# More seven-product pairs in a SwiGLU on Trainium2, with activation sums kept in DRAM

## The chip, the cores and the metric

The kernel runs on one core of one Trainium2 chip. The metric is device time in microseconds (us). The kernel before takes 2040.8 us, the median of three runs (2040.3 to 2041.55). Lower is better. A profile was taken of one more execution.

The engines have short names here: PE is TensorE (matmuls), PEld its weight loads, DVE is VectorE, ACT is ScalarE, POOL is GpSimd and SP is the engine that issues most DMAs. All five run their own instructions in the order in which the program put them there, and wait for each other through semaphores.

## What is computed

A two-layer encoder on 256 tokens of width 2048, with 256 memory tokens. Each layer has a token mixer (a gated MLP in layer 0, attention in layer 1), attention into the memory, an output projection, and a dense SwiGLU of inner width 5632. Everything is float32. The change touches the SwiGLU alone:

```python
D_MODEL = 2048; SEQ = 256; DEPTH = 2; D_FF = 5632
def swiglu(h, w_gate_up, w_down):
    gate, up = jnp.split(h @ w_gate_up, 2, axis=-1)
    return (jax.nn.silu(gate) * up) @ w_down
def reference(...):
    for l in range(DEPTH):
        ...
        x = x + jnp.concatenate([tok_out, mem_out], axis=-1) @ w_out[l]
        x = x + swiglu(rms_norm(x, g_ffn[l]), w_gate_up[l], w_down[l])
    return x
```

## The kernel before

**Precision.** PE multiplies in fp32r, a shortened float32. To keep precision, each operand is split into a high and a low part, `hi` and `lo`: ACT makes `hi` by a cast (L254 for weights), DVE makes `lo` by a subtraction (L255). Each product of a 128-row block is then three matmuls (`matmul3`, L198 to L200): hi by hi, lo of the activations by hi, hi by lo of the weights.

**Pairs.** In the feed-forward stage a `Pair` computes two blocks of 512 output columns at once for both halves of the tokens. For gate/up the two blocks are gate and up of one block `f` of the inner width (11 of them, "pair f"), for down they are two neighbouring blocks of the output (two pairs, `jj` = 0 and 1, for each chunk of the inner width). A pair runs over units: a unit `i` covers two blocks of 128 features, so gate/up has 8 units, down 8 (or 6 in the last chunk). Its weights, four tiles of 128x512, come in as `raw` by two DMAs of SP (L357).

**Eight or seven products.** A unit is a 2x2 by 2x2 product of blocks. `eight` does it with 8 products, 24 matmuls. `seven` does it with 7 products, 21 matmuls, as Strassen's method does (in Winograd's form). For this it needs sums of weights, which DVE forms in `prepare` (L347 to L350, four additions, the three new ones in a tile `T`) and which are split too (a second pair of `whi` and `wlo`, of 1536 elements), and sums of activations (`activation_sums`, L300 to L308: four short DVE instructions and a split). At the end of the last seven of a pair, `inner` combines four PSUM banks (a copy on ACT and four DVE additions, L397 to L401; in down four more, L405). At the end of the last unit, `outer` adds the other four banks (L413, two after each half of the tokens).

**Which units are seven.** In gate/up units 0, 1 and 2 of the features (`fast`, L743), two of them in pair 0 and three in all others; their activation sums are made once a layer and lie in SBUF. In down the units in `quick` (L762): two in the first two chunks for either `jj`, and in the last chunk none in layer 0 and one in layer 1. The lists `order` say where in the pair the sevens stand: with three sevens in gate/up they are units one, three and five of eight.

**What sets the order.** The code issues unit after unit and prepares one unit ahead (`run`, L327 to L337). Other work is put in by a queue of delays, `later` and `tick` (L96 to L112), one tick for each half unit: the transposes and splits of the SwiGLU output (`turn_a`), the residuals and so on. A scheduler then orders the instructions of each engine. There are three buffers of `whi` and three of `wlo` (`W_TILES`), four of `raw`, four PSUM banks `acc` and four `m`, and 26 tiles `a` for activations, sums and products in the feed-forward stage (`FFN_TILES`).

Of the kernel before, what the change touches and what calls it, by code (L numbers as in the profile page):

```python
# [10 lines left out]
F32 = mybir.dt.float32  # L11
F32R = mybir.dt.float32r
AF = mybir.ActivationFunctionType
ALU = mybir.AluOpType
AX = mybir.AxisListType

P = 128
# [10 lines left out]
NB = 512  # L28
# [3 lines left out]
KC4 = 4  # L32
# [4 lines left out]
KC3 = 3  # L37


class Parts:  # L40
# [8 lines left out]
    def get(self, kc, t):  # L49
        return self.ap[kc, t]  # L50
# [3 lines left out]
def encoder(ctx: ExitStack, tc: tile.TileContext, x, mem, g_mix, g_ffn, w_in_a, g_v_a, w_spatial, b_spatial,  # L54
            w_in_b, g_q_b, g_k_b, g_mem, w_mem_kv, g_mq, g_mk, w_out, w_gate_up, w_down, rope_c, rope_s, out):
    nc = tc.nc
# [7 lines left out]
    dram = ctx.enter_context(tc.tile_pool(name="dram", bufs=1, space=bass.MemoryType.DRAM))  # L64
# [6 lines left out]
    def nm(s):  # L71
        uid[0] += 1
        return f"{s}_{uid[0]}"

    def big(dt=F32, shape=None):
        return room["p"].tile(shape or [P, NB], dt, tag="a", name=nm("a"))

    def small(n, long=False):
        return sp.tile([P, n], F32, tag=f"{'r' if long else 's'}{n}", name=nm(f"s{n}"), bufs=8 if long else 6)

    def misc():
        return psm.tile([P, NB], F32, tag="m", name=nm("m"))

    def v4(a):
        return a.rearrange("p (c n) -> p c n", n=P)
# [10 lines left out]
    def later(delay, fn):  # L96
        queue.append((clock[0] + delay, len(queue), fn))

    def tick():
        clock[0] += 1  # L100
        run_due(clock[0])
# [86 lines left out]
    def split(src, shape):  # L188

        hi = big(F32R, shape)  # L190
        lo = big(F32R, shape)
        nc.scalar.copy(hi, src)  # L192
        nc.vector.tensor_tensor(lo, src, hi.bitcast(F32), ALU.subtract)  # L193
        return hi, lo
# [7 lines left out]
    def transpose4(src, dst):  # L202
        for c in range(4):
            nc.tensor.transpose(dst[:, c * P:(c + 1) * P], src[:, c * P:(c + 1) * P], ident)  # L204
# [27 lines left out]
    class Norm:  # L232


        def __init__(self):
            self.ss = [small(8, long=True) for _ in range(NT)]
# [11 lines left out]
    def halves(raw, n, step=KC4):  # L248

        hi = wp.tile([P, KC4, NB], F32R, tag="whi", name=nm("whi"))[:, :n]  # L250
        lo = wp.tile([P, KC4, NB], F32R, tag="wlo", name=nm("wlo"))[:, :n]
        for c in range(0, n, step):
            cut = slice(c, min(c + step, n))
            nc.scalar.copy(hi[:, cut], raw[:, cut])  # L254
            nc.vector.tensor_tensor(lo[:, cut], raw[:, cut], hi[:, cut].bitcast(F32), ALU.subtract)  # L255
        return [(hi[:, c, :], lo[:, c, :]) for c in range(n)]
# [43 lines left out]
    def activation_sums(a0, a1):  # L300

        q = big(F32, [P, 4, P])
        nc.vector.tensor_tensor(q[:, 0], a1[:, 0], a1[:, 1], ALU.subtract)
        nc.vector.tensor_tensor(q[:, 2], a1[:, 0], a0[:, 0], ALU.subtract)
        nc.vector.tensor_tensor(q[:, 1], a0[:, 0], q[:, 0], ALU.subtract)
        nc.vector.tensor_tensor(q[:, 3], a0[:, 1], q[:, 1], ALU.subtract)
        hi, lo = split(q, [P, 4, P])
        return [(hi[:, i, :], lo[:, i, :]) for i in range(4)]  # L308

    class Pair:  # L310

# [27 lines left out]
        def prepare(self, i):  # L339

            if i in self.ready:
                return
            raw = self.fetch(i)
            self.ready[i] = (raw,)
            if i in self.fast:
                T = room["p"].tile([P, KC3, NB], F32, tag="T", name=nm("T"), bufs=2)
                nc.vector.tensor_tensor(raw[:, 0], raw[:, 0], raw[:, 1], ALU.add)  # L347
                nc.vector.tensor_tensor(T[:, 0], raw[:, 0], raw[:, 3], ALU.add)
                nc.vector.tensor_tensor(T[:, 1], T[:, 0], raw[:, 1], ALU.subtract)
                nc.vector.tensor_tensor(T[:, 2], T[:, 0], raw[:, 2], ALU.add)  # L350
                self.ready[i] = raw, T

        def fetch(self, i):
# [11 lines left out]
            matmul3(self.bank[name], a, b, self.part[name] == 1, self.part[name] == self.of.get(name, self.most))  # L365

        def seven(self, i, raw, T):
            t1, w00, w10, w11 = halves(raw, KC4)
            t2, t3, t4 = halves(T, KC3)
            get, (q5, s2, q7, q3) = self.parts.get, self.sums[i]  # L370
            k0, k1 = 2 * i, 2 * i + 1
            inner = [(1, get(k0, 0), w00), (5, q5, t1), (6, s2, t2), (7, q7, t3)]
            outer = [(2, get(k1, 0), w10), (3, q3, w11), (4, get(k1, 1), t4)]
            if self.bank:
                inner, outer = inner[:1] + outer[:2], inner[1:] + outer[2:]
            for some in (inner, outer):
                for name, a, b in some:
                    self.add(name, a, b)
                tick()
# [225 lines left out]
    for l in range(DEPTH):  # L605
# [105 lines left out]
        else:  # L711
# [12 lines left out]
            for c in range(3):  # L724
                acc = linear(hT, w, c * NB)
                attend(head_norm(acc, norm.r, ghead["q"], True), (5, 6, 10, 13), lambda: own["k"], lambda: own["v"],
                       lambda h, c=c: (4 * c + h) // 3, 4 * c, cat)
# [12 lines left out]
        scope = ExitStack()  # L740
        room["p"] = scope.enter_context(tc.tile_pool(name=f"ffn{l}", bufs=FFN_TILES, reuse_waits="tile"))
        sums = {}
        fast = (0, 1, 2)  # L743

        def feature_sums(i):
            j, c = i // 2, 2 * (i % 2)
            whole = []
            for t in range(NT):
                hi, lo = hF.whole[j, t]
                a = big(F32, [P, 2, P])  # L750
                nc.vector.tensor_tensor(a, hi[:, c:c + 2].bitcast(F32), lo[:, c:c + 2].bitcast(F32), ALU.add)
                whole.append(a)
            sums[i] = activation_sums(*whole)

        for i in fast:
            later(2 + 2 * i, lambda i=i: feature_sums(i))

        hT = Parts()
        next_norm = Norm()
        for chunk in (range(0, 4), range(4, 8), range(8, 11)):  # L760
            aT, aS, half = Parts(), {}, {}
            quick = [2 * f + 1 for f in chunk[:2 if chunk[-1] < 10 else l]]  # L762

            def turn_a(a, t, f, aT=aT, aS=aS, half=half, quick=quick):
                tp = misc()
                transpose4(a, tp)
                hi, lo = split(v4(tp), [P, 4, P])
                for i in range(4):
                    aT.put(4 * f + i, t, hi[:, i, :], lo[:, i, :])
                i = 2 * f + 1  # L770
                if i in quick:
                    half[i, t] = big(F32, [P, 2, P])
                    nc.scalar.copy(half[i, t], v4(tp)[:, 2:4])
                    if t == NT - 1:
                        aS[i] = activation_sums(half[i, 0], half[i, 1])

            pairs = {}
            for f in chunk:
                order, some = ((3, 4, 5, 0, 6, 1, 7, 2), 2) if f == 0 else ((0, 3, 1, 4, 2, 5, 6, 7), 3)
                pairs[f] = Pair(hF, sums, w_gate_up[l], f * NB, DFF + f * NB, order, fast[:some])  # L780
            for f, g in pairs.items():
                g.run(pairs.get(f + 1))
                for t in range(NT):
                    a = kp.tile([P, NB], F32, tag="sg", name=nm("sg"), bufs=2)
                    nc.scalar.activation(a, g.out[t][0], AF.Silu, scale=norm.r[t])
                    nc.vector.scalar_tensor_tensor(a, g.out[t][1], norm.r[t], a, ALU.mult, ALU.mult)
                    later(3 + t if f == chunk[-1] else 12 + t, lambda a=a, t=t, f=f: turn_a(a, t, f))
            last = chunk[-1] == 10
            every = [2 * f + c for f in chunk for c in range(2)]
            slow = [i for i in every if i not in quick]  # L790
            pairs = []
            for jj in range(2):
                order = list(slow)
                for n, i in enumerate(quick):
                    order.insert(2 * n + (0 if jj and not last else 2), i)
                into = [[X[t][2 * jj + n] for n in range(2)] for t in range(NT)]
                pairs.append(Pair(aT, aS, w_down[l], 2 * jj * NB, (2 * jj + 1) * NB, order, quick, into))
            for jj, g in enumerate(pairs):
                g.run(None if jj else pairs[1])
                for j in (2 * jj, 2 * jj + 1):  # L800
                    if last and l < DEPTH - 1:
                        residual_turns(j, next_norm, gslice("mix", l + 1), hT)
                    elif last:
                        for t in range(NT):
                            parts = 2 if j == 3 and t == NT - 1 else 1
                            for i in range(parts):
                                cs = slice(i * NB // parts, (i + 1) * NB // parts)
                                eng = nc.scalar if i else nc.sync
                                eng.dma_start(out[0, t * P:(t + 1) * P, j * NB + cs.start:j * NB + cs.stop],
                                              X[t][j][:, cs])  # L810
# [37 lines left out]
```

## Time and profile before

| | |
|---|---|
| median of 3 runs | 2040.8 us (2040.3 to 2041.55) |
| span of the profiled execution | 2038.5 us |
| HBM read / written | 390.26 MB / 4.19 MB |
| granted PE clock | 1.000 |
| weight units split on DVE (2048 elements) | 264 |
| halves T split on DVE (1536 elements) | 82 |

The span runs from the first to the last instruction of the profiled execution; nothing else of that execution is timed, so its own time stands beside the median by the span alone, 2.3 us shorter. In the rows of the profile a group reads: line, engine, operation, output<-input, shapes, count | busy us in all, mean ns of one | idle time of its engine ahead of it and what ended it. In rows of a timeline the first two numbers are start and duration in us. In rows of waits: who <- whom: us in all, times, the longest.

### The profile page before, as it was taken

Reading aid. Unit: us, or ns where it says so; the run is one execution under the profiler, and the core shown is the slowest. Engines: PE = TensorE matmul, PEld = TensorE weight load, DVE = VectorE, ACT = ScalarE, POOL = GpSimd, SP = SyncE. Lnnn points to the kernel's source line nnn. Section 1 sums busy time; section 2 is a strip of 40 time slices with the busy share of each in tenths; the row PEclk is TensorE's granted clock in tenths of the full one; section 3 lists DMA queues with packets and bytes.
Section 4 is the critical chain, followed back from the end, with each engine's and each line's share of the span. In section 5 each row is a group of like instructions: output and inputs, shape, how many; then the busy total and the mean of one; then the engine's idle time right before and its main releaser. Section 6 shows DMA issues by size and latency. Waiting matters only on the chain.

```text
span 2038.5 us, 24693 instructions
## 1 busy us (share of the span) xinstructions
PE 2027.7 (99%) x9298; PEld 1679.9 (82%) x9298; DVE 1605.0 (79%) x1862; ACT 1095.0 (54%) x1389; POOL 50.6 (2%) x80
## 2 busy tenths in 40 slices
PE   9999999999999999999999999999999999999999
PEld 7888888888888888888888888888888888888887
DVE  5675557998879988887566886589979899798876
ACT  7765455454445554444555765555544455444552
POOL 2010000000000000000010100000000000000000
PEclk9999999999999999999999999999999999999999
DMA  9754554646656465665566544555566555565554
GB/s 325 253 179 155 185 188 154 227 165 206 203 190 227 165 207 196 202 227 194 186 198 204 173 133 141 202 185 178 195 206 218 195 184 190 205 221 192 183 197 137
DMA packets 202432, 396.08 MB, mean 194 GB/s; under 512 B 11068, under 2 KB 11432, under 8 KB 202312
## 3 DMA queue, kind: packets, MB, share of 16 engines
q1 hardware_dynamic: 198800, 385.79, 56.6%
q0 software_dynamic: 2048, 6.42, 1.0%
q10 hardware_dynamic: 1464, 2.28, 0.3%
q8 instruction: 73, 1.20, 0.2%
q14 instruction: 47, 0.39, 0.1%
HBM read 390.26 MB, written 4.19 MB: 194 GB/s over the span
## 4 chain that ended last, share of the span: by engine, by line
PE 96%; DVE 3%; DMA 1%; issue 1%; ACT 0%; SPq 0%; DVEq 0%; ACTq 0%
PE acc L200 27%; PE acc L199 27%; PE acc L198 27%; PE m L200 4%; PE m L198 4%; PE m L199 4%; PE m L204 2%; DVE wlo L255 1%; DMA raw<-in_w_gate_up 1%; PE m L500 0%; PE m L643 0%; ACT whi L254 0%; DVE x L413 0%; DVE e L413 0%; DMA x<-in_x 0%
## 5 line engine op out<-in xcount | busy, mean ns | idle before, releaser
L254 ACT CAST whi<-raw 128x2048 fp32r<-128x2048 f32 (+2 forms) x465 | 700.8, 1539 | 585.0 <-PE acc L199 512.5
L255 DVE TENSOR_TENSOR wlo<-raw,whi 128x2048 fp32r<-128x2048 f32 (+2 forms) x465 | 836.4, 1823 | 223.9 <-ACT whi L254 220.1
L198 PE MATMUL acc<-whi,h 128*128 128x512 f32 x1440 | 563.7, 392 | 0.0
L199 PE MATMUL acc<-whi,h 128*128 128x512 f32 x1440 | 562.6, 391 | 0.0
L200 PE MATMUL acc<-wlo,h 128*128 128x512 f32 x1440 | 524.1, 392 | 0.9 <-DVE wlo L255 0.9
L198 PE MATMUL acc<-whi,a 128*128 128x512 f32 x1062 | 414.8, 391 | 0.0
L199 PE MATMUL acc<-whi,a 128*128 128x512 f32 x1062 | 414.2, 390 | 0.0
L200 PE MATMUL acc<-wlo,a 128*128 128x512 f32 x1062 | 398.2, 391 | 0.0
L200 PEld LDWEIGHTS acc<-wlo,h 128*128 128x128 f32 x1440 | 270.6, 188 | 56.6 <-DVE wlo L255 1.5
L199 PEld LDWEIGHTS acc<-whi,h 128*128 128x128 f32 x1440 | 270.7, 188 | 55.3
L198 PEld LDWEIGHTS acc<-whi,h 128*128 128x128 f32 x1440 | 271.0, 188 | 54.0
L200 PEld LDWEIGHTS acc<-wlo,a 128*128 128x128 f32 x1062 | 199.4, 188 | 41.3 <-DVE wlo L255 0.3
L199 PEld LDWEIGHTS acc<-whi,a 128*128 128x128 f32 x1062 | 199.5, 188 | 40.4
L198 PEld LDWEIGHTS acc<-whi,a 128*128 128x128 f32 x1062 | 199.5, 188 | 40.2
L254 ACT CAST whi<-T 128x1536 fp32r<-128x1536 f32 x82 | 121.4, 1480 | 143.8 <-PE acc L199 102.2
L255 DVE TENSOR_TENSOR wlo<-T,whi 128x1536 fp32r<-128x1536 f32 x82 | 143.5, 1750 | 39.1 <-ACT whi L254 39.0
L198 PE MATMUL m<-whi,a 128*128 128x512 f32 x264 | 104.2, 395 | 0.7 <-ACT whi L254 0.7
L199 PE MATMUL m<-whi,a 128*128 128x512 f32 x264 | 102.9, 390 | 0.0
L347 DVE TENSOR_TENSOR raw<-raw 128x512 f32<-128x512 f32 x82 | 56.1, 684 | 54.9 <-DMA raw<-in_w_gate_up 53.5
L200 PE MATMUL m<-wlo,a 128*128 128x512 f32 x264 | 89.6, 389 | 0.0
L192 ACT CAST a<-m 128x512 fp32r<-128x512 f32 x80 | 46.7, 587 | 42.8 <-PE m L204 31.7
L193 DVE TENSOR_TENSOR a<-m,a 128x512 fp32r<-128x512 f32 x80 | 53.8, 682 | 13.1 <-ACT a L192 12.9
(126 smaller groups left out, 1473.1 us busy)
## 6 DMA issues: line engine op xcount, KB each, us to landing
raw<-in_w_gate_up SPq DMA_DIRECT2D x352, 512.0 KB, 4.7
raw<-in_w_down SPq DMA_DIRECT2D x176, 512.0 KB, 5.2
raw<-in_w_out SPq DMA_DIRECT2D x32, 1024.0 KB, 5.1
raw<-in_w_in_a SPq DMA_DIRECT2D x24, 1024.0 KB, 5.2
raw<-in_w_in_b SPq DMA_DIRECT2D x24, 1024.0 KB, 5.1
raw<-in_w_mem_kv SPq DMA_DIRECT2D x16, 1024.0 KB, 5.1
raw<-in_w_in_a SPq DMA_DIRECT2D x7, 512.0 KB, 6.2
x<-in_x SPq DMA_DIRECT2D x8, 256.0 KB, 5.8
```

The lines of the kernel that those rows point to most:

```text
L192: nc.scalar.copy(hi, src)
L193: nc.vector.tensor_tensor(lo, src, hi.bitcast(F32), ALU.subtract)
L198: nc.tensor.matmul(out, lhsT=a[0], rhs=b[0], start=start, stop=False)
L199: nc.tensor.matmul(out, lhsT=a[1], rhs=b[0], start=False, stop=False)
L200: nc.tensor.matmul(out, lhsT=a[0], rhs=b[1], start=False, stop=stop)
L204: nc.tensor.transpose(dst[:, c * P:(c + 1) * P], src[:, c * P:(c + 1) * P], ident)
L254: nc.scalar.copy(hi[:, cut], raw[:, cut])
L255: nc.vector.tensor_tensor(lo[:, cut], raw[:, cut], hi[:, cut].bitcast(F32), ALU.subtract)
L347: nc.vector.tensor_tensor(raw[:, 0], raw[:, 0], raw[:, 1], ALU.add)
```

## The change

- Gate/up has a fourth unit of seven products, i = 3 (`fast`), which pairs 2, 5, 7 and 9 use (`many`); they then alternate seven and eight to the end, `(0, 4, 1, 5, 2, 6, 3, 7)`. The others keep their two or three.
- Down has three sevens for `jj` = 1 in the first two chunks (`some`), and one in the last chunk for `jj` = 0 (in layer 1 for both). In all 13 units more are sevens.
- The activation sums of gate/up are written to DRAM when they are made (`spilt`), by POOL's DMA queue, and read back into new tiles during the second half of down, for the next chunk (`reload_sums`).
- The sums of weights take three DVE instructions in place of four: one of 2x512 elements and two of 512 (now L352 to L354). The products 5 and 6 change places in `inner` of `seven`.

```diff
+    class Quarters(list):
+        def __init__(self, hi, lo):
+            self.tiles = hi, lo
+            super().__init__((hi[:, i, :], lo[:, i, :]) for i in range(4))
...
             if i in self.fast:
                 T = room["p"].tile([P, KC3, NB], F32, tag="T", name=nm("T"), bufs=2)
-                nc.vector.tensor_tensor(raw[:, 0], raw[:, 0], raw[:, 1], ALU.add)
-                nc.vector.tensor_tensor(T[:, 0], raw[:, 0], raw[:, 3], ALU.add)
-                nc.vector.tensor_tensor(T[:, 1], T[:, 0], raw[:, 1], ALU.subtract)
-                nc.vector.tensor_tensor(T[:, 2], T[:, 0], raw[:, 2], ALU.add)
+                w01 = raw[:, 0].unsqueeze(1).to_broadcast([P, 2, NB])
+                nc.vector.tensor_tensor(T[:, :2], raw[:, 1:4:2], w01, ALU.add)
+                nc.vector.tensor_tensor(raw[:, 0], T[:, 0], raw[:, 3], ALU.add)
+                nc.vector.tensor_tensor(T[:, 2], raw[:, 0], raw[:, 2], ALU.add)
                 self.ready[i] = raw, T
...
         def seven(self, i, raw, T):
-            t1, w00, w10, w11 = halves(raw, KC4)
-            t2, t3, t4 = halves(T, KC3)
+            t2, w00, w10, w11 = halves(raw, KC4)
+            t1, t3, t4 = halves(T, KC3)
...
-            inner = [(1, get(k0, 0), w00), (5, q5, t1), (6, s2, t2), (7, q7, t3)]
+            inner = [(1, get(k0, 0), w00), (6, s2, t2), (5, q5, t1), (7, q7, t3)]
...
-        fast = (0, 1, 2)
+        fast = (0, 1, 2, 3)
+        spilt = [[dram.tile([P, NB], F32, name=f"sum_{l}_{i}_{h}") for h in range(2)] for i in fast]
...
             sums[i] = activation_sums(*whole)
+            for h in range(2):
+                nc.gpsimd.dma_start(spilt[i][h], sums[i].tiles[h].rearrange("p c n -> p (c n)").bitcast(F32))
+
+        def reload_sums(i):
+            hi, lo = big(F32R, [P, 4, P]), big(F32R, [P, 4, P])
+            for a, b in zip((hi, lo), spilt[i]):
+                nc.gpsimd.dma_start(a.rearrange("p c n -> p (c n)").bitcast(F32), b)
+            sums[i] = Quarters(hi, lo)
...
+        many = {0: 2, 2: 4, 5: 4, 7: 4, 9: 4}
         for chunk in (range(0, 4), range(4, 8), range(8, 11)):
+            last = chunk[-1] == 10
             aT, aS, half = Parts(), {}, {}
-            quick = [2 * f + 1 for f in chunk[:2 if chunk[-1] < 10 else l]]
+            quick = [2 * f + 1 for f in chunk[:1 if last else 3]]
...
-                order, some = ((3, 4, 5, 0, 6, 1, 7, 2), 2) if f == 0 else ((0, 3, 1, 4, 2, 5, 6, 7), 3)
+                some = many.get(f, 3)
+                order = {2: (3, 4, 5, 0, 6, 1, 7, 2), 3: (0, 3, 1, 4, 2, 5, 6, 7), 4: (0, 4, 1, 5, 2, 6, 3, 7)}[some]
...
             for jj in range(2):
-                order = list(slow)
-                for n, i in enumerate(quick):
+                some = quick[:1 - jj * (l == 0) if last else 2 + jj]
+                order = [i for i in every if i not in some]
+                for n, i in enumerate(some):
...
             for jj, g in enumerate(pairs):
+                if jj and not last:
+                    for i in fast:
+                        later(4 + 2 * i, lambda i=i: reload_sums(i))
                 g.run(None if jj else pairs[1])
```

The first place is the change from pair 9 to pair 10 of gate/up in layer 0. DVE before: from the `lo` of pair 9's last unit, `wlo_7076`, on; `wlo_7117` and `wlo_7121` are the two halves of pair 10's first unit, L399 to L401 combine pair 9, L413 closes it:

```order
L255 TENSOR_TENSOR wlo_7076<-raw_7027,whi_7075 128x2048
L399 TENSOR_TENSOR e_6980<-m_6817,e_6979 128x512
L193 TENSOR_TENSOR a_7024<-m_7018,a_7023 128x512
L255 TENSOR_TENSOR wlo_7117<-raw_7067,whi_7116 128x2048
L400 TENSOR_TENSOR e_6979<-m_6825,e_6979 128x512
L401 TENSOR_TENSOR e_6981<-m_6825,e_6980 128x512
L193 TENSOR_TENSOR a_7052<-m_7046,a_7051 128x512
L347 TENSOR_TENSOR raw_7152<-raw_7152 128x512
L413 TENSOR_TENSOR e_6978<-acc_6829,e_6978 128x512
L255 TENSOR_TENSOR wlo_7121<-T_7070,whi_7120 128x1536
L348 TENSOR_TENSOR T_7155<-raw_7152 128x512
L413 TENSOR_TENSOR e_6980<-acc_6833,e_6980 128x512
```

DVE now at that place. Ahead of these rows stand five: `wlo_7168`, the `lo` of pair 9's last unit, a sum of weights (L352), `wlo_7209`, the first half of pair 10's first unit, L402, which starts to combine pair 9, and a second sum (L353). `wlo_7213` is the other half of pair 10's first unit, `wlo_7252` its second unit:

```order
L255 TENSOR_TENSOR wlo_7213<-T_7163,whi_7212 128x1536
L193 TENSOR_TENSOR a_7094<-m_7088,a_7093 128x512
L403 TENSOR_TENSOR e_7153<-m_6898,e_7152 128x512
L417 TENSOR_TENSOR e_7151<-acc_6906,e_7151 128x512
L354 TENSOR_TENSOR T_7247<-raw_7244 128x512
L255 TENSOR_TENSOR wlo_7252<-raw_7205,whi_7251 128x2048
L352 TENSOR_TENSOR T_7315<-raw_7312 128x1024
L404 TENSOR_TENSOR e_7152<-m_6902,e_7152 128x512
L405 TENSOR_TENSOR e_7154<-m_6902,e_7153 128x512
L193 TENSOR_TENSOR a_7125<-m_7119,a_7124 128x512
L353 TENSOR_TENSOR raw_7312<-T_7315,raw_7312 128x512
L417 TENSOR_TENSOR e_7152<-acc_6914,e_7152 128x512
```

All four combining additions (L402 to L405) and `wlo_7252` of the second unit now stand in front of the second closing one, L417 on `acc_6914`; before, the combining had begun a unit earlier.

PE now at the same place: the last product of the second unit's first group is `acc_7232`, then come the products with the half T (`m_7224`, `m_7228`), then `acc_7236`, whose bank is the one that L417 on `acc_6914` reads last:

```order
L200 MATMUL acc_7232<-wlo_7252,h_2431 128x512
L198 MATMUL m_7224<-whi_7212,a_6360 128x512
L199 MATMUL m_7224<-whi_7212,a_6361 128x512
L200 MATMUL m_7224<-wlo_7213,a_6360 128x512
L198 MATMUL m_7228<-whi_7212,a_6360 128x512
L199 MATMUL m_7228<-whi_7212,a_6361 128x512
L200 MATMUL m_7228<-wlo_7213,a_6360 128x512
L198 MATMUL acc_7236<-whi_7208,a_6360 128x512
```

The second unit's products on `acc_7232` moved ahead of the first unit's half T; before, they stood behind the whole first unit.

The second place is the change from pair 7 of gate/up into down, layer 0. DVE now, the last twelve of 17 rows that begin with `wlo_5940` (pair 7's last unit); `wlo_5984`, `wlo_6023` and `wlo_6072` are down's first three:

```order
L255 TENSOR_TENSOR wlo_6023<-raw_5980,whi_6022 128x2048
L193 TENSOR_TENSOR a_5873<-m_5867,a_5872 128x512
L403 TENSOR_TENSOR e_5932<-m_5677,e_5931 128x512
L417 TENSOR_TENSOR e_5930<-acc_5685,e_5930 128x512
L354 TENSOR_TENSOR T_6018<-raw_6015 128x512
L255 TENSOR_TENSOR wlo_6072<-raw_6015,whi_6071 128x2048
L352 TENSOR_TENSOR T_6107<-raw_6104 128x1024
L404 TENSOR_TENSOR e_5931<-m_5681,e_5931 128x512
L405 TENSOR_TENSOR e_5933<-m_5681,e_5932 128x512
L193 TENSOR_TENSOR a_5904<-m_5898,a_5903 128x512
L353 TENSOR_TENSOR raw_6104<-T_6107,raw_6104 128x512
L417 TENSOR_TENSOR e_5931<-acc_5693,e_5931 128x512
```

DVE before, from pair 7's last unit, `wlo_5876`, on:

```order
L255 TENSOR_TENSOR wlo_5876<-raw_5835,whi_5875 128x2048
L398 TENSOR_TENSOR e_5787<-m_5629,e_5786 128x512
L399 TENSOR_TENSOR e_5788<-m_5625,e_5787 128x512
L255 TENSOR_TENSOR wlo_5920<-raw_5913,whi_5919 128x2048
L400 TENSOR_TENSOR e_5787<-m_5633,e_5787 128x512
L401 TENSOR_TENSOR e_5789<-m_5633,e_5788 128x512
L193 TENSOR_TENSOR a_5832<-m_5826,a_5831 128x512
L347 TENSOR_TENSOR raw_5951<-raw_5951 128x512
L193 TENSOR_TENSOR a_5860<-m_5854,a_5859 128x512
L348 TENSOR_TENSOR T_5954<-raw_5951 128x512
L413 TENSOR_TENSOR e_5786<-acc_5637,e_5786 128x512
```

Three units of down are now split ahead of the closing additions, where one was.

More of the change, by code (lines that the diff above doesn't have):

```diff
@@ L306, in activation_sums @@
         nc.vector.tensor_tensor(q[:, 3], a0[:, 1], q[:, 1], ALU.subtract)
-        hi, lo = split(q, [P, 4, P])
-        return [(hi[:, i, :], lo[:, i, :]) for i in range(4)]
+        return Quarters(*split(q, [P, 4, P]))
+    class Quarters(list):
+        def __init__(self, hi, lo):
+            self.tiles = hi, lo
+            super().__init__((hi[:, i, :], lo[:, i, :]) for i in range(4))
     class Pair:
@@ L787, in encoder @@
                     later(3 + t if f == chunk[-1] else 12 + t, lambda a=a, t=t, f=f: turn_a(a, t, f))
-            last = chunk[-1] == 10
             every = [2 * f + c for f in chunk for c in range(2)]
-            slow = [i for i in every if i not in quick]
             pairs = []
             for jj in range(2):
-                order = list(slow)
-                for n, i in enumerate(quick):
+                some = quick[:1 - jj * (l == 0) if last else 2 + jj]
+                order = [i for i in every if i not in some]
+                for n, i in enumerate(some):
                     order.insert(2 * n + (0 if jj and not last else 2), i)
                 into = [[X[t][2 * jj + n] for n in range(2)] for t in range(NT)]
-                pairs.append(Pair(aT, aS, w_down[l], 2 * jj * NB, (2 * jj + 1) * NB, order, quick, into))
+                pairs.append(Pair(aT, aS, w_down[l], 2 * jj * NB, (2 * jj + 1) * NB, order, some, into))
             for jj, g in enumerate(pairs):
+                if jj and not last:
+                    for i in fast:
+                        later(4 + 2 * i, lambda i=i: reload_sums(i))
                 g.run(None if jj else pairs[1])
```

## The prediction

> **What bounds the kernel now.** First the page: busy shares, and the chain of work that ended last by engine.
>
> ```profile
> PE 2027.7 (99%) x9298; PEld 1679.9 (82%) x9298; DVE 1605.0 (79%) x1862; ACT 1095.0 (54%) x1389; POOL 50.6 (2%) x80
> ...
> PE 96%; DVE 3%; DMA 1%; issue 1%; ACT 0%; SPq 0%; DVEq 0%; ACTq 0%
> ```
>
> TensorE (PE) is busy nearly throughout, but a busy PE need not be at its peak. So next the waits of PE alone:
>
> ```profile
> PE m L134 <- DMA gst_mix<-in_g_mix: 4.3, 1, 4.3
> PE acc L200 <- DVE wlo L255: 0.9, 1, 0.9
> PE m L198 <- ACT whi L254: 0.7, 4, 0.2
> PE m L204 <- DMA x<-in_x: 0.3, 1, 0.3
> ```
>
> It waits 6.2 us in all, 4.3 of them at the start. The timeline of PE gives its pace, and what four transposes of `turn_a` cost:
>
> ```profile
> 361.16 0.39 PE L198 MATMUL acc<-whi,h 128*128 128x512 f32 x1
> 361.38 0.39 PE L199 MATMUL acc<-whi,h 128*128 128x512 f32 x1
> 361.61 0.39 PE L198 MATMUL acc<-whi,h 128*128 128x512 f32 x1
> 361.84 0.39 PE L199 MATMUL acc<-whi,h 128*128 128x512 f32 x1
> ...
> 908.30 0.60 PE L204 MATMUL m<-ident,sg 128*128 128x128 f32 x4
> 908.65 0.48 PE L198 MATMUL acc<-whi,h 128*128 128x512 f32 x1
> 908.96 0.39 PE L199 MATMUL acc<-whi,h 128*128 128x512 f32 x1
> ```
>
> Starts lie 0.68 us apart over three matmuls: 0.227 us each; the 0.39 us overlap. From the transposes to the second matmul behind them it is 0.66 us, so four transposes cost 0.43. So the kernel is PE-bound, and a matmul left out is worth 0.227 us, if VectorE (DVE) keeps up. That it hardly does in the feed-forward stage, the sums by stretches of 20 us show (length, then busy time of PE, PEld, DVE, ACT, POOL):
>
> ```profile
> 400.00:420.00 20.00, 20.00 (x92) 16.56 (x91) 20.00 (x25) 9.12 (x10) 0.00 (x0) 1.00 0.48 159
> 420.00:440.00 20.00, 20.00 (x92) 16.57 (x91) 15.75 (x14) 12.11 (x9) 0.00 (x0) 1.00 0.56 198
> 440.00:460.00 20.00, 20.00 (x92) 16.42 (x91) 20.00 (x27) 11.18 (x10) 0.00 (x0) 1.00 0.55 177
> ```
>
> DVE has 55.75 of 60 us. The share of 79% is a mean with the mixers. Now its timeline where pair 9 of gate/up gives way to pair 10 in layer 0 (the closing adds of pair 9 are L413, and here L399 to L401 still combine it):
>
> ```profile
> 908.69 0.68 DVE L399 TENSOR_TENSOR e<-m,e 128x512 f32<-128x512 f32 x1
> 909.29 0.68 DVE L193 TENSOR_TENSOR a<-m,a 128x512 fp32r<-128x512 f32 x1
> 909.89 2.28 DVE L255 TENSOR_TENSOR wlo<-raw,whi 128x2048 fp32r<-128x2048 f32 x1
> 912.09 0.68 DVE L400 TENSOR_TENSOR e<-m,e 128x512 f32<-128x512 f32 x1
> 912.69 0.68 DVE L401 TENSOR_TENSOR e<-m,e 128x512 f32<-128x512 f32 x1
> ...
> 915.46 1.75 DVE L255 TENSOR_TENSOR wlo<-T,whi 128x1536 fp32r<-128x1536 f32 x1
> 917.13 0.68 DVE L348 TENSOR_TENSOR T<-raw 128x512 f32<-128x512 f32 x1
> ```
>
> One instruction follows another. By the starts, an operation of 512 elements takes 0.60 us, of 1536 1.67, of 2048 2.20; their mean durations (rows below) are 0.08 longer, since ends overlap starts. So 128x1024, with a mean of 1.22, takes 1.14, 256 about 0.33 and 128 about 0.20, on the same line.
>
> ```profile
> L255 DVE TENSOR_TENSOR wlo<-raw,whi 128x2048 fp32r<-128x2048 f32 x264 | 599.5, 2285 | 105.5 <-ACT whi L254 104.5
> L254 ACT CAST whi<-raw 128x2048 fp32r<-128x2048 f32 x264 | 499.9, 1914 | 482.4 <-PE acc L199 427.9 <-issue 39.0 <-DVE T L348 4.4
> L255 DVE TENSOR_TENSOR wlo<-raw,whi 128x1024 fp32r<-128x1024 f32 x199 | 235.5, 1220 | 116.5 <-ACT whi L254 113.7 <-PE acc L200 1.7 <-PE m L204 0.7
> L254 ACT CAST whi<-T 128x1536 fp32r<-128x1536 f32 x82 | 121.4, 1480 | 143.8 <-PE acc L199 102.2 <-PE m L199 31.1 <-DVE T L350 7.0
> ```
>
> The casts wait for PE to release a `whi` (427.9 us): there are three, a pair of seven products takes two. So DVE cannot work ahead at will: a `wlo` starts at the earliest when PE is done with the `whi` three back, plus the cast (1.91 or 1.48 us). From there DVE must do everything up to what PE needs next, in order.
>
> **What goes.** 13 pairs lose 3 of 24 matmuls each: 39 x 0.227 = **8.85 us**, on the path. Pairs per layer: gate/up 32 to 36; down 8 to 11 (layer 0) and 10 to 12 (layer 1).
>
> **What comes on DVE.** 13 halves of T: 13 x 1.67 = 21.7 us. Weight sums: before 82 x 4 x 0.60 = 196.8, now 95 x (1.14 + 2 x 0.60) = 222.3. Seven more activation sums of 4 x 0.20 + 0.60 = 1.4 us: 9.8; a fourth input to them, 4 x 0.33 = 1.3; one more combining in down, 8 x 0.60 = 4.8. Together 63 us, in stretches where DVE already has 93%, with 8.85 us less of PE to lie beside. A pair of gate/up with four sevens holds 4 x 2.20 + 4 x 2.20 + 4 x 1.67 + 4 x 2.34 = 33.6 us of weights on DVE, and combining, SwiGLU, splits and an activation sum (4 + 4 + 2 + 2 times 0.60 or so, + 1.4) 8.6: 42.2 us. PE has 4 x 21 + 4 x 24 = 180 matmuls and 8 transposes, 41.7 us. DVE is over PE, and it isn't spread evenly.
>
> **Where it stops PE.** In a pair with four sevens the last seven is unit 7 of 8, so the four combining adds (L402 to L405) and the four closing ones (L417) meet at the change of pairs, in front of what PE needs: the sixth of the next pair's first seven products (`acc_7236`) needs the PSUM bank that the second L417 frees (first place in the orders above). I add up, from the start of `wlo_7168`: 17 instructions, 3 x 2.20 + 1.67 + 2 x 1.14 + 11 x 0.60 = 17.15 us. PE has from the release to that product 63 matmuls and 8 transposes, 15.16 us, less the cast 1.91: 13.25. Short by **3.9 us**. It is the same behind pairs 2, 5 and 9, in both layers: 6 x 3.9 = 23.4.
> Behind pair 7 (into down, second place, from `wlo_5940`): 4 x 2.20 + 2 x 1.14 + 11 x 0.60 = 17.68 against 57 matmuls and 8 transposes, 13.80 - 1.91 = 11.89: 5.8 us, twice: 11.6.
> Start of the feed-forward stage, where the fourth activation sum lies among pair 0's work: 4 x 2.20 + 2 x 1.67 + 2 x 1.14 + 9 x 0.60 + 2 x 0.33 + 4 x 0.20 = 21.3 against 90 matmuls, 20.4 - 1.48 = 18.9: 2.4, twice: 4.8.
> From the first half of down into the second, where now three sevens come: 5 x 2.20 + 2 x 1.67 + 3 x 1.14 + 14 x 0.60 = 26.2 against 119 and 117 matmuls less 1.48, 25.5 and 25.0: 0.7 and 1.2, twice: 3.8.
> Sum 43.6 us in 14 stretches that don't overlap. Hand-overs come on top:
>
> ```profile
> 906.93 0.39 PE L199 MATMUL acc<-whi,h 128*128 128x512 f32 x1
> 907.16 0.39 PE L200 MATMUL acc<-wlo,h 128*128 128x512 f32 x1
> ...
> 907.36 1.92 ACT L254 CAST whi<-raw 128x2048 fp32r<-128x2048 f32 x1 [2.84 <-PE acc L199]
> ```
>
> The cast starts 0.20 us after the matmul behind the last use; with 0.08 for the end of the last DVE instruction, 0.28 x 14 = 3.9. I take 47.5 us; bounds: 35 (the two large kinds alone) to 67 (a whole us more at each, and 5 us at each start, where weights come late too). The same sums over the order of before find no stretch that is short, and its trace has no such wait. The three-instruction sum saves 0.06 us a pair, but `raw[:, 0]` is ready 1.14 us later; that lies in the sums.
>
> **The spill.** Per layer 8 stores and 16 loads of 256 KB on POOL's queue.
>
> ```profile
> a<-in_mem POOLq DMA_DIRECT2D x8, 256.0 KB, 8.5
> ```
>
> Such a load lands after 8.5 us; at least 240 matmuls (54 us) lie between the last release that a reload of i = 0 to 2 waits for and its first use. Queued behind a waiting reload are only reloads, and loads of the next layer. SP's queue keeps its order. The transfers are 12.6 MB beside 396: I take nothing; at 194 GB/s the 4.2 MB of stores would be 22 us if nothing hid them, below nothing there is no reason. Does POOL's issuing hold up DVE?
>
> ```profile
> 835.29 0.79 POOL L156 DMA_DIRECT2D a<-in_rope_c  x1 [504.28 <-DVE raw L347]
> 836.08 0.74 POOL L156 DMA_DIRECT2D a<-in_rope_s  x1
> ...
> 835.74 0.68 DVE L348 TENSOR_TENSOR T<-raw 128x512 f32<-128x512 f32 x1
> 836.46 0.69 DVE L349 TENSOR_TENSOR T<-T,raw 128x512 f32<-128x512 f32 x1
> ```
>
> Beside two issues of 0.77 us, a sum started 0.72 instead of 0.60 us after the one before: 0.06 an issue, 3 us of DVE for 48 issues, most of them in down, where DVE has room. I take nothing for it. [...]
>
> **Sum.** Own span 2038.5 - 8.85 + 47.5 = 2077.2; the median of the runs lies 2.3 above the span (2040.8): **2079.5, say 2080 us**.
>
> **Rivals.** *The cover holds*: DVE's lead in the buffers outlasts the changes of pairs and only the matmuls count: 2040.8 - 8.9 = 2032, **faster**. For it speak 79% on DVE and a before without stalls; against it that three `whi` bound the lead. It decides if the stretches' shortage of 43.6 stays under 8.85 us: the counts would have to be wrong by 35. *Half the stalls*: some of the closing adds are off the path: 2040.8 - 8.9 + 22 = 2054. *Late weights*: DVE frees `raw` late, transfers of 4.7 to 5.2 us then start late and each shortage grows, or the stores hold up the weights: 2080 + 22 = 2102. [...] *The change doesn't do what it says*: the order has 39 matmuls less, so this has no weight.
>
> **Numbers.** Forecast 0.76, cover holds 0.10, half 0.06, late weights 0.05, POOL 0.03. The forecast's own bounds are 2040.8 - 8.85 + 35 = 2067 to 2099. The range takes in part of the half case: 2058 to 2099. 0.2%, 4 us, is about what a measurement tells from no change here: faster 0.10; same 0.02, out of the half case; slower 0.88.
>
> **What would show it.** PE's waits: L198 on DVE L417 and L200 on L255, 3 to 6 us at the change behind pairs 2, 5, 7 and 9, together about 45. DVE without a gap in those stretches, 128x1024 sums of 1.2 us; its busy time up by 60. No PE wait for a reload. If PE waits for nothing and the span falls by 9, the stretches are wrong; if PE waits for `raw`, the third rival is right.

## The result and the profile after

The changed kernel takes **2092.8 us** (median, 2090.8 to 2094.4), the kernel before 2040.6 beside it: a ratio of 1.0254, 95% interval 1.0242 to 1.0266. The forecast was 2080 with a range of 2058 to 2099. The profiled execution has a span of 2091.0 us. Its busy shares and its chain by engine:

```profile
PE 2037.8 (97%) x9259; PEld 1676.3 (80%) x9259; DVE 1665.5 (80%) x1879; ACT 1120.6 (54%) x1420; POOL 82.9 (4%) x128
...
PE 90%; DVE 5%; issue 2%; DMA 1%; ACT 1%; SPq 0%; DVEq 0%; ACTq 0%
```

PE has 39 matmuls less, yet is busy 10.1 us longer than before (2027.7); DVE has 60.5 us more (1605.0 before). The waits of PE, which were 6.2 us in all:

```profile
PE acc L200 <- DVE wlo L255: 10.8, 11, 3.2
PE acc L198 <- DVE e L417: 9.8, 4, 3.2
PE m L198 <- ACT a L788: 9.6, 6, 1.6
PE m L198 <- DVE e L405: 6.8, 6, 1.1
PE m L198 <- ACT whi L254: 5.4, 4, 1.4
```

These five come to 42.4 us, less than the span grew by, with the matmuls gone on top. Part of the rest is in the clock. Two stretches of 20 us at the start of layer 0's feed-forward stage (length, then busy time and matmuls of PE, then PEld, DVE, ACT, POOL, the granted clock, DMA):

```profile
360.00:380.00 20.00, 16.73 (x60) 12.91 (x60) 19.93 (x25) 8.74 (x8) 1.08 (x2) 0.83 0.62 219
380.00:400.00 20.00, 20.00 (x92) 16.55 (x91) 13.68 (x10) 12.57 (x9) 0.00 (x0) 1.00 0.49 162
```

The granted clock was 0.83 there on average, and 60 matmuls ran where 92 do. PE's timeline inside that stretch (start, duration):

```profile
369.73 0.40 PE L200 MATMUL m<-wlo,a 128*128 128x512 f32 x1
373.29 0.80 PE L200 MATMUL acc<-wlo,h 128*128 128x512 f32 x1 [3.16 <-DVE wlo L255]
373.88 0.63 PE L198 MATMUL acc<-whi,h 128*128 128x512 f32 x1
374.31 0.63 PE L199 MATMUL acc<-whi,h 128*128 128x512 f32 x1
...
378.57 0.63 PE L200 MATMUL acc<-wlo,h 128*128 128x512 f32 x1
379.00 0.47 PE L198 MATMUL acc<-whi,h 128*128 128x512 f32 x1
379.31 0.40 PE L199 MATMUL acc<-whi,h 128*128 128x512 f32 x1
```

PE waits 3.16 us for a `wlo`, and then its matmuls start 0.43 us apart in place of 0.227 for 5.1 us; from 373.90 to 379.00 the granted clock was 0.50. To size each place, every start of a matmul is compared with 0.227 us after the one before it; "lost" below is what a place has over that, wait and slow matmuls together, where it is over 0.4 us, from 300 us on. Before lost 3.9 us in this way, after 63.0. The difference, 59.1, less 8.85 for the 39 matmuls, is 50.3 of the 52.5 us by which the span grew.

| place, both layers | forecast | lost | of it slow matmuls |
|---|---|---|---|
| behind pairs 2, 5, 9 (six) | 25.1 | 25.6 | 0 |
| pair 7 into down (two) | 12.2 | 15.2 | 4.4 |
| start of the stage (two) | 5.4 | 11.9 | 4.4 |
| first into second half of down (four) | 4.9 | 6.5 | 0 |
| four places not forecast | 0 | 3.9 | 0 |

(Forecast with 0.28 for each hand-over.) Of the 3.9 us that before lost, 2.8 lie at the start of the stage too. At the four places that were not forecast, where down gives way to the next gate/up, DVE stood idle just ahead for 4.5 to 5.9 us, because the sum at the head of its queue (L352) needed a `raw` that had not landed. The split that PE then waited for stood behind this sum, so there the weights came late.

Behind pair 7 the two layers differ. In layer 0 it lost 6.2 us, close to the 6.1 of the forecast: the slow matmuls (1.6 us) stand between two waits for L417, on a DVE that runs without a gap, so the second wait took them up and they cost nothing. In layer 1 they stand behind the last wait, and it lost 9.0.

The first place of the orders above, behind pair 9 in layer 0, on DVE:

```profile
931.19 2.29 DVE L255 TENSOR_TENSOR wlo<-raw,whi 128x2048 fp32r<-128x2048 f32 x1 [1.57 <-ACT whi L254]
...
934.54 2.28 DVE L255 TENSOR_TENSOR wlo<-raw,whi 128x2048 fp32r<-128x2048 f32 x1
936.74 0.69 DVE L402 TENSOR_TENSOR e<-m,e 128x512 f32<-128x512 f32 x1
...
939.61 0.68 DVE L193 TENSOR_TENSOR a<-m,a 128x512 fp32r<-128x512 f32 x1
940.21 0.68 DVE L403 TENSOR_TENSOR e<-m,e 128x512 f32<-128x512 f32 x1
940.81 0.68 DVE L417 TENSOR_TENSOR e<-acc,e 128x512 f32<-128x512 f32 x1
...
942.00 2.28 DVE L255 TENSOR_TENSOR wlo<-raw,whi 128x2048 fp32r<-128x2048 f32 x1
...
945.94 0.68 DVE L405 TENSOR_TENSOR e<-m,e 128x512 f32<-128x512 f32 x1
...
947.74 1.88 DVE L417 TENSOR_TENSOR e<-acc,e 128x512 f32<-128x512 f32 x3
```

and on PE:

```profile
941.24 0.50 PE L198 MATMUL m<-whi,h 128*128 128x512 f32 x1 [1.59 <-ACT a L788]
...
944.34 0.50 PE L200 MATMUL acc<-wlo,h 128*128 128x512 f32 x1 [0.31 <-DVE wlo L255]
...
946.68 0.50 PE L198 MATMUL m<-whi,a 128*128 128x512 f32 x1 [1.14 <-DVE e L405]
...
948.48 0.49 PE L198 MATMUL acc<-whi,a 128*128 128x512 f32 x1
```

From the split at 931.19 on, DVE runs without a gap while PE stops three times. The prediction's 17 instructions, up to the second L417 (the first of the three at 947.74), take 17.15 us here, to the hundredth what it summed, and PE's product on the bank that this L417 frees starts at 948.48, 0.06 us after its end. So the stretch and its size, 4.27 us, are as forecast; the names of the waits are not. PE meets the `m` banks first. It stops for the copy L788 on ACT (of the transposes of the SwiGLU output), which stood behind a cast of weights on ACT, then for the late split, then for L405. When it comes to the bank of the last L417, little is left to wait for.

### The profile page after: what moved, and what is told of

The parts are those of the page before. It is cut to its first block, busy times and chain, and to the rows that moved or that the text cites. A ratio compares the mean times of both kernels' runs of the same rounds, so it can differ in the third digit from the quotient of the medians.

```text
span 2091.0 us, 24823 instructions
## 1 busy us (share of the span) xinstructions
PE 2037.8 (97%) x9259; PEld 1676.3 (80%) x9259; DVE 1665.5 (80%) x1879; ACT 1120.6 (54%) x1420; POOL 82.9 (4%) x128
## 4 chain that ended last, share of the span: by engine, by line
PE 90%; DVE 5%; issue 2%; DMA 1%; ACT 1%; SPq 0%; DVEq 0%; ACTq 0%
PE acc L200 25%; PE acc L198 25%; PE acc L199 25%; PE m L198 4%; PE m L199 4%; PE m L200 4%; DVE wlo L255 2%; PE m L204 2%; DMA raw<-in_w_gate_up 1%; ACT whi L254 1%; DVE T L352 1%; PE m L504 0%; DVE a L193 0%; DVE e L417 0%; DVE T L354 0%
## 5 line engine op out<-in xcount | busy, mean ns | idle before, releaser
L198 PE MATMUL acc<-whi,h 128*128 128x512 f32 x1392 | 545.7, 392 | 0.1
L199 PE MATMUL acc<-whi,h 128*128 128x512 f32 x1392 | 544.4, 391 | 0.0
L200 PE MATMUL acc<-wlo,h 128*128 128x512 f32 x1392 | 511.2, 394 | 9.7 <-DVE wlo L255 9.5
L199 PEld LDWEIGHTS acc<-whi,h 128*128 128x128 f32 x1392 | 262.2, 188 | 54.2
L198 PEld LDWEIGHTS acc<-whi,h 128*128 128x128 f32 x1392 | 262.7, 189 | 52.7 <-ACT whi L254 0.5
L198 PEld LDWEIGHTS acc<-whi,a 128*128 128x128 f32 x1045 | 197.6, 189 | 52.5 <-DVE e L417 12.7
L254 ACT CAST whi<-T 128x1536 fp32r<-128x1536 f32 x95 | 140.8, 1482 | 143.2 <-PE acc L199 112.6
L255 DVE TENSOR_TENSOR wlo<-T,whi 128x1536 fp32r<-128x1536 f32 x95 | 166.4, 1752 | 48.9 <-ACT whi L254 48.9
L352 DVE TENSOR_TENSOR T<-raw 128x1024 f32<-128x1024 f32 x95 | 115.8, 1219 | 60.3 <-DMA raw<-in_w_gate_up 60.3
L198 PE MATMUL m<-whi,a 128*128 128x512 f32 x308 | 122.4, 397 | 12.7 <-DVE e L405 6.8
L199 PE MATMUL m<-whi,a 128*128 128x512 f32 x308 | 120.0, 390 | 0.0
L200 PE MATMUL m<-wlo,a 128*128 128x512 f32 x308 | 107.3, 390 | 0.0
L198 PEld LDWEIGHTS m<-whi,a 128*128 128x128 f32 x308 | 57.8, 188 | 31.6 <-DVE e L405 10.5
L200 PEld LDWEIGHTS m<-wlo,a 128*128 128x128 f32 x308 | 57.8, 188 | 12.1
```

Source lines behind the costliest of these rows:

```text
L198: nc.tensor.matmul(out, lhsT=a[0], rhs=b[0], start=start, stop=False)
L199: nc.tensor.matmul(out, lhsT=a[1], rhs=b[0], start=False, stop=False)
L200: nc.tensor.matmul(out, lhsT=a[0], rhs=b[1], start=False, stop=stop)
L352: nc.vector.tensor_tensor(T[:, :2], raw[:, 1:4:2], w01, ALU.add)
```

## Experiments

Every kernel ran beside the kernel before on the same chip. Two theories stood against each other at first: by the **order theory** time is lost only where DVE's queue holds more in front of what PE waits for than PE has work to cover; by the **load theory** each microsecond of DVE that is added in this stage counts, wherever it stands (60 us were added, 59 lost).

### The parts alone: sums3, spill_sums, no_fours

`sums3` is before with the change's `prepare` and the exchange of products 5 and 6.

> Before with the sums of weights in three instructions and products 5 and 6 exchanged, nothing else. Order theory (time is lost only where DVE's queue holds more in front of what PE waits for than PE has work to cover it): the built order has no stretch that becomes short, so 2040 to 2042 us, as before. Load theory (each us of DVE in the feed-forward stage counts, wherever it stands): 82 x 0.06 = 4.9 us less of DVE, so 2036.

2042.4 us, ratio 1.0010 (1.0001 to 1.0019). The smaller load of DVE (4.9 us expected, 7.7 by its busy time, 1605.0 to 1597.2) brought nothing, rather a loss: PE lost 5.7 us against 3.9.

`spill_sums` adds the stores and reloads, with `fast = (0, 1, 2)`, no pair on four sevens and `quick` as before.

> The same with three activation sums a layer written to DRAM and read back (12 stores and 24 loads of 256 KB), but no further unit made a seven. The prediction took nothing for the spill: 2040 to 2042. Rival: in the built order the reloads let PE's products at the change from the first to the second half of down stand 2 to 30 places earlier, in the four places where the profile of after shows 1.5 us before an L198 on m; then 4 x 1.4 and a cast of a T, 2046. Traffic theory (stores and loads on POOL's queue hold up the weights or DVE): up to 2062, and waits for raw or longer DVE instructions.

2044.5, ratio 1.0023 (1.0013 to 1.0032); PE lost 8.2 us. PE's waits on casts, here in `spill_sums`:

```profile
PE m L198 <- ACT whi L254: 5.8, 6, 1.4
```

and in `sums3`:

```profile
PE m L198 <- ACT whi L254: 1.3, 6, 0.2
```

The four losses of 1.63 at the change of halves of down are there, to the hundredth as in after, with two sevens in the second half as before. So they belong to the spill and not to the third seven. In `sums3` the same four places lose 0.5 each, so the spill adds 1.1 each, 4.5 us of the 6.5.

`no_fours` is after without pairs of four sevens:

```diff
-        many = {0: 2, 2: 4, 5: 4, 7: 4, 9: 4}
+        many = {0: 2}
```

> After with no pair of gate/up on four sevens (the fourth sum is still made, stored and reloaded, down as in after). Order theory: 6 x 4.27 behind pairs 2, 5 and 9 and 6.2 + 9.0 behind pair 7 go, 24 matmuls come (5.4): 2092.8 - 40.8 + 5.4 = 2057, and up to 2063 if the smaller waits of down grow. Load theory: 8 x (1.67 + 2.34) = 32 us less of DVE: 2061. This run sizes the fours; order_f tells the theories apart.

2055.9, ratio 1.0073 (1.0057 to 1.0090). Eight units are 37 of the 52 us, though each saves three matmuls. PE still loses 20.2 us, 12.4 of them at the start of the stage.

### The same work in another order: order_f

```diff
-                order = {..., 4: (0, 4, 1, 5, 2, 6, 3, 7)}[some]
+                order = {..., 4: (0, 4, 1, 2, 5, 3, 6, 7)}[some]
```

> After with the order (0, 4, 1, 2, 5, 3, 6, 7) in the pairs with four sevens: the last seven is the sixth unit in place of the eighth, so that the four combining adds lie two units ahead of the closing ones. DVE and PE do the same work. Order theory: the stalls of 4.27 behind pairs 2, 5, 9 nearly go, pair 7 keeps some; from the sums over its order 2066 (2058 to 2074). Load theory: 2093, unchanged.

**2056.9**, ratio 1.0081 (1.0066 to 1.0096): 36 us less than after, with the same instructions (DVE is busy 1664.2 us, in after 1665.5). The load theory has fallen. DVE at the same change of pairs:

```profile
919.01 0.68 DVE L402 TENSOR_TENSOR e<-m,e 128x512 f32<-128x512 f32 x1
...
921.00 0.68 DVE L403 TENSOR_TENSOR e<-m,e 128x512 f32<-128x512 f32 x1
...
924.48 0.68 DVE L404 TENSOR_TENSOR e<-m,e 128x512 f32<-128x512 f32 x1
925.07 0.68 DVE L405 TENSOR_TENSOR e<-m,e 128x512 f32<-128x512 f32 x1
925.67 0.68 DVE L417 TENSOR_TENSOR e<-acc,e 128x512 f32<-128x512 f32 x1
...
928.00 0.68 DVE L417 TENSOR_TENSOR e<-acc,e 128x512 f32<-128x512 f32 x1
928.60 0.68 DVE L193 TENSOR_TENSOR a<-m,a 128x512 fp32r<-128x512 f32 x1
929.20 1.27 DVE L417 TENSOR_TENSOR e<-acc,e 128x512 f32<-128x512 f32 x2
```

From L403 to the end of the last L417 it takes 9.5 us here, 9.4 in after. But in after a split of 2048 (at 942.00) stands between the first and the last L417; here none does, the combining begins a unit earlier, and the next split comes when the banks are free. PE loses nothing over 0.4 us behind pairs 2, 5 and 9. Behind pair 7, 6.4 us of the 15.2 stay. The gain is above the forecast of 27, and the time 1 us below the range that was expected: the 25.6 us behind pairs 2, 5 and 9 went entirely, the slow matmuls behind pair 7 shrank with the wait (PE waits 4.1 us for L417 in all, 9.8 in after), and two of the four losses in down fell from 1.63 to 0.5.

### The start, pair 7 and the clock: late_fourth, pair7_three, clock_gaps

`late_fourth` issues the fourth activation sum behind a sum of weights on DVE (`mark[0]`, the latest L352):

```diff
-        for i in fast:
+        for i in fast[:3]:
             later(2 + 2 * i, lambda i=i: feature_sums(i))
+        def fourth():
+            with tc.issue_after(mark[0].ins):
+                feature_sums(3)
+        later(26, fourth)
```

> After with the fourth activation sum of gate/up moved behind pair 1 on DVE (pair 2 is the first to need it). In after the start of the feed-forward stage lost 3.7 us in a wait and 2.9 in slow matmuls behind it in layer 0, 3.8 and 1.5 in layer 1. If the slow matmuls belong to the wait: 2092.8 - 11.9 = 2081. If the low clock there has another cause and stays: 2092.8 - 7.5 = 2085. As the prediction had it (2.7 each): 2087.

2080.7, ratio 1.0199 (1.0182 to 1.0216): 12.1 us less than after, near the 11.9 of waits and slow matmuls together. In the trace the start loses 1.7 us, where after loses 11.9, and the changes behind pairs 2 and 7 some 3 us less. The sum did not land behind pair 1, as expected: in layer 0 it starts at 370.64, behind the closing adds of pair 0, in after at 356.93, ahead of them. The stretch that had a clock of 0.83:

```profile
360.00:380.00 20.00, 19.70 (x86) 15.69 (x85) 20.00 (x23) 10.69 (x8) 0.00 (x0) 1.00 0.55 194
```

The move did not make DVE earlier. In layer 0 the split for which PE waited in after ended at 373.23 there; here, with its lines one further down, it ends at 374.19, and PE first uses it at 374.91:

```profile
371.91 2.28 DVE L256 TENSOR_TENSOR wlo<-raw,whi 128x2048 fp32r<-128x2048 f32 x1
374.91 0.40 PE L201 MATMUL acc<-wlo,h 128*128 128x512 f32 x1
```

In after that product was next in line at 369.96. Here the scheduler put it behind some 5 us of other products. The order of PE is the other half of the sum that the prediction made, and it moved with the place of one sum on DVE.

`pair7_three` is after with `many = {0: 2, 2: 4, 5: 4, 9: 4}`.

> After with pair 7 of gate/up on three sevens. In after the change from pair 7 into down lost 6.2 us in layer 0 and 9.0 in layer 1, 10.2 of them in waits and 5.0 in slow matmuls; 6 matmuls come back (1.4). Waits and clock go together: 2092.8 - 15.2 + 1.4 = 2079; waits alone: 2084; load theory, 2 x 4.0 us less of DVE: 2085.

2077.2, ratio 1.0179 (1.0164 to 1.0195): 15.6 us. Here too the slow matmuls went with the wait: PE has no wait for L417 left (9.8 us in after), and the mean granted clock of the profiled execution is 0.998 (0.995 in after).

`clock_gaps` gives DVE needless work in the kernel before (`gap` is 16, 20 and 26 instructions for pairs 1, 5 and 9):

```diff
+                if n == 0 and t == 0 and not self.into:
+                    for _ in range(gap[self.na // NB]):
+                        nc.vector.tensor_tensor(o[0][0], o[0][0], o[0][0], ALU.max)
```

> Before with 16, 20 and 26 additional DVE instructions (max of a tile with itself, so the result stays) ahead of the closing adds of pairs 1, 5 and 9 of gate/up in both layers. They make PE wait several times for 0.5 to 6 us. In after, waits up to 2.0 us between two matmuls were followed by matmuls 0.227 us apart, waits of 3.3 to 3.6 by 7 to 14 matmuls 0.427 us apart, and of two waits of 2.7 one. Clock theory: waits of 3.4 and more are followed by 7 to 15 slow matmuls each time (1.4 to 3 us), waits under 2 by none. Rival: the low clock belongs to those places of after (to the spill's DMAs or to the change into down): then none here.

2101.0 us (one run). The longest wait, behind pair 9, on PE:

```profile
967.01 0.39 PE L201 MATMUL acc<-wlo,h 128*128 128x512 f32 x1
973.71 0.80 PE L199 MATMUL acc<-whi,h 128*128 128x512 f32 x1 [6.31 <-DVE e L417]
974.30 0.63 PE L200 MATMUL acc<-whi,h 128*128 128x512 f32 x1
...
978.57 0.62 PE L201 MATMUL acc<-wlo,h 128*128 128x512 f32 x1
978.99 0.42 PE L199 MATMUL acc<-whi,h 128*128 128x512 f32 x1
```

Eleven matmuls lie 0.43 us apart, as they did at the granted clock of 0.50 in after, without a spill and in another place, so the rival has fallen: the slow matmuls come behind a wait here too. Two waits with 2.4 us between starts (2.0 us idle) were each followed by seven slow matmuls, those of 2.0 and 2.1 by none; in after, one of two with 2.7 was. So 2.4 us were enough here, and 2.2 in one place of `all13_mended`, while one wait of 2.7 was not; what decides it between 2.2 and 2.7 was not shown.

### The spill's order, and a pace that changed: spill_held, spill_held64, pad_all

`spill_held` is `spill_sums` with the reloads behind a small POOL instruction that reads what the combining makes (shortened):

```diff
+    hold_ = kp.tile([P, 1], F32, name='hold_', bufs=1)
...
+                    def reload_all():
+                        mark[1] = nc.gpsimd.tensor_copy(hold_, held[0][:, :1])
+                        with tc.issue_after(mark[1].ins):
+                            for i in fast:
+                                reload_sums(i)
+                    later(10, reload_all)
```

> spill_sums with the reloads issued behind a small POOL instruction that reads what the combining of down's second half makes; the same bytes move, only later, and the built order at the change of halves is that of sums3 again. If the order made the difference of 2 us between spill_sums and sums3: 2042 and no 1.5 us wait there; if the traffic made it: 2044.5 as spill_sums.

2067.2, ratio 1.0130 (1.0115 to 1.0146): neither. The losses of 1.63 are gone from the trace (0.46 is left of each), and PE lost 3.8 us in all, as before. PE's matmuls stand at the change of halves in exactly the order of `sums3`, which those of `spill_sums` don't. So the order theory holds for the waits; the same bytes cost no wait when the order is the old one. But the matmuls themselves became slower, so the next two runs looked for the reason.

> spill_held again, with the small POOL tile 64 bytes wide in place of 4 (padded to 32). In spill_held PE lost nothing in waits, and the matmuls with an activation from the a tiles as weights lay 0.233 us apart in place of 0.227: 4000 or so of them, 25 us. The a, T, e and sg tiles lay 32 bytes further than in every other kernel, the weights and h did not. If their place did it: back to 0.227 and 2042 (the reloads' place in the order is then the 2 us between spill_sums and sums3). If the POOL instruction or the held reloads did it: 2067 again.

2067.4, ratio 1.0133 (1.0118 to 1.0148). The matmuls in groups by operands, here in `spill_held64` (its lines are three further down):

```profile
L201 PE MATMUL acc<-whi,h 128*128 128x512 f32 x1440 | 564.1, 392 | 0.2 <-ACT whi L257 0.2
...
L201 PE MATMUL acc<-whi,a 128*128 128x512 f32 x1062 | 421.0, 397 | 0.0
```

and in `sums3`:

```profile
L198 PE MATMUL acc<-whi,h 128*128 128x512 f32 x1440 | 563.7, 392 | 0.0
...
L198 PE MATMUL acc<-whi,a 128*128 128x512 f32 x1062 | 415.0, 392 | 0.0
```

Only those with an activation from an `a` tile are longer: 397 against 392 ns, and by their starts 0.233 against 0.227 us, in about 4000 of them, some 24 of the 25.6 us between the two spans. Some are so from the beginning of the program, long before the added instruction runs for the first time, at 560.71 (in the first 330 us the median from start to start is 0.231 us, against 0.227). The granted clock is 1.0.

> sums3 with an unused tile of 32 bytes ahead of all others, so that every tile moves by 32 bytes, weights and activations alike. If what slows a matmul is that its two operands differ in their place modulo 64 bytes: 2042, as sums3. If it is a place at a multiple of 64 bytes itself: 2067 or more, since all matmuls are then slow. If neither: 2042, and spill_held64 decides.

2043.1, ratio 1.0014 (1.0005 to 1.0023), as `sums3`. With every tile moved by 32 bytes the matmuls with an `a` tile take 392 ns, so a place at a multiple of 64 bytes is not the reason; and whether the `a` tiles are moved against the weights by 32 or by 64 bytes makes no difference (2067.2 and 2067.4). What remains is that the added tile moves the `a` tiles against the tiles of the weights, which `pad_all` doesn't do; that was not tried without the added instruction, and stays open.

### All 13 mended, and the best combination: all13_mended, three_fours

Both have the order of `order_f`, the late fourth sum and the held reloads, and so the slower matmuls too. `three_fours` has four sevens in pairs 3, 5 and 8, and the sums of weights and down of before.

> All 13 sevens of after, with the order of order_f, the fourth sum behind pair 1, and the reloads held as in spill_held64. Order theory: of the 59 us lost, 36 go by the order, 10 by the fourth sum's place and 4 to 6 at the change of halves; what is left by the sums over the order is 2050 (2045 to 2055), slower than before. Load theory: 2093. If the mends don't add up, because each only uncovers the next wait: 2056 or more, as order_f.

2073.4, ratio 1.0160 (1.0143 to 1.0177). PE lost 17.5 us in place of 63.0; the rest of what was expected is hidden by the pace of the matmuls. Even without that the 8.85 us of 39 matmuls would not have paid for 17.5, against 3.9 before (and slower matmuls give DVE more time, so at the old pace the loss would hardly be smaller). PE's largest waits:

```profile
PE acc L203 <- DVE wlo L258: 5.9, 7, 1.5
...
PE acc L201 <- DVE e L421: 3.2, 3, 1.8
```

> The best combination found by adding up built orders: four sevens in pairs 3, 5 and 8 in the order of order_f, the fourth sum behind pair 1, reloads held, sums of weights in four instructions and down as in before: 18 matmuls less (4.1 us), 1 to 2 us of small waits more. Order theory: 2038 (2036 to 2041), the same as before or faster by 0.1%. Load theory: 6 x 4.1 us more of DVE: 2060.

2064.7, ratio 1.0120 (1.0105 to 1.0135). PE lost 3.7 us, no more than before, with 18 matmuls (4.1 us) less. At this pace, which leaves DVE more time, the order is free of stops; whether it is so at the old pace, and the kernel then faster than before, was not measured. No kernel here beat the one before.

## Why the prediction was right, and where its sizes were off

- **The stretches.** The step that sums DVE's queue between the release of a `whi` and what PE needs next held: behind pairs 2, 5 and 9 it gave 25.1 us, measured 25.6; `order_f` shows that it is the place of the adds, not their number. The wait was named wrongly in part (the banks `m` and a copy on ACT come first, not the last L417).
- **Pair 7 and the start of the stage.** The mechanism held (`pair7_three` 15.6 us, `late_fourth` 12.1, the latter by PE's order as much as by DVE's queue). The terms 12.2 and 5.4 were too small, because a wait of PE was priced by its length alone: slow matmuls came behind four waits, 8.8 us. Those of layer 0 behind pair 7 were taken up by the next wait; the other 7.2 are more than half of the 12.8 us by which the forecast fell short. At the start the waits were longer as well, 7.5 against 5.4, and the 3.9 us of late weights had no term.
- **First into second half of down.** The term 4.9 came near to 6.5 by luck, since its reason, the third seven, was wrong: `spill_sums` has the same four losses without it. They come with the reloads, but for the 0.5 each that `sums3` has too.
- **The spill.** "I take nothing" was right for the traffic and for POOL's issuing: PE waits for no reload in after, and `spill_held` moves the same bytes without the four losses. It was wrong for the order: the step said that queued behind a waiting reload are only reloads, but it didn't compare how the scheduler then places PE's products at the change of halves. This term is 4.5 of the 6.5 us of the row above, not one beside it; in `spill_sums` the whole spill is worth 2.1 us over `sums3`.
- **The three-instruction sum.** Its 0.06 us a pair brought nothing: `sums3` is 1.0010 of before, interval 1.0001 to 1.0019. Its small losses are up to 0.8 us a place; in four of these places the split that PE waits for stands behind the first of the three, which takes 1.14 us where the first of four took 0.60. That this, or the later `raw[:, 0]`, is the reason is argued, not shown.
- **What came on DVE.** 63 us were worked out, 60.5 measured.
- **The rivals.** *The cover holds* fell with 59 us lost; *half the stalls* likewise. *Late weights* gives 2102; they are there, but with 3.9 us and not with 22. That POOL's issues hold up DVE (0.03 in the forecast) did not show: in after, eleven additions of 512 elements ran beside an issue of the spill, and the next instruction started 0.60 us after each of them, as without an issue; and `spill_sums`, with 36 of the 48 issues, is only 2.1 us above `sums3`.

## What to carry to other kernels

Before a saving on the bound engine is counted, sum the queue of the engine that feeds it between the moment a buffer comes free and the next product that needs it; that sum is decided by the order, and here one unit's place in a list was worth 36 us, the work being the same. In these runs a wait of TensorE with 2.2 us or more between starts was followed, all but once, by 1.4 to 3 us of slow matmuls, and shorter ones by none, so one long wait can be dearer than two short ones. They cost only where no further wait for the same queue took them up: behind pair 7 layer 0, with such a wait, lost 6.2 us, layer 1, without, 9.0. After adding even a tile of a few bytes, compare the start-to-start time of the matmuls (0.233 against 0.227 us here) as well as the waits.

## What the runs showed of the hardware that was not expected

- TensorE's half clock after short waits: starts 2.4 us apart were followed by seven matmuls at 0.43 us in `clock_gaps`, twice, and 3.6 us apart by six to twelve in after, at a granted clock of 0.50.
- Matmuls with an activation from the `a` tiles, which an added tile had moved by 32 or 64 bytes, took 0.233 in place of 0.227 us (2.6%, 25 us of the span) at a granted clock of 1.0; moving all tiles by 32 bytes changed nothing (2043.1 against 2042.4). The cause is open.
